# A short-band attention branch whose two key blocks are joined before the softmax and parted again behind the transposes

## The chip, the cores and the metric

The kernel runs on one NeuronCore of one Trainium2 chip. The metric is the device time of one execution in microseconds (us), the median of several runs. A profile of one further execution shows what each engine did when: TensorE (PE, with its weight loads as PEld), VectorE (DVE), ScalarE (ACT), GpSimd (POOL) and the DMA queue of SyncE (SP).

## What is computed

One decoder layer over 1024 tokens of width 1024. It has two attention mixers beside each other: mixer A (three branches, long) and mixer B, the short band: 8 query heads over 2 key heads, head width 64, a causal window of 128 keys, ALiBi and one sink per head. The change is in mixer B alone. Cut to that, the reference is:

```python
def banded_attention(q, k, v, slopes, window, sinks):      # window = 128, Q_BLOCK = 128
    # a block of 128 queries sees its own 128 keys and the 128 before them
    s = einsum('bgrnqd,bgnkd->bgrnqk', qb, kb) * (dh ** -0.5)
    dist = qpos[:, :, None] - kpos[:, None, :]
    valid = (dist >= 0) & (dist < window) & (kpos[:, None, :] >= 0)
    s = s - slopes * dist
    s = where(valid, s, NEG)
    p = softmax(concatenate([s, sink], axis=-1), axis=-1)[..., :-1]
    return einsum('bgrnqk,bgnkd->bgrnqd', p, vb)
```

With a window of exactly 128, query p of a block sees key j of its own block where j <= p, and key j of the block ahead where j > p. For each j exactly one of the two is seen: 128 keys in all, in 256 columns of which half are masked.

## The kernel before

All products are made in float32 from a rounded high part and a low part (names `..h` and `..l`, or `wh`, `wl`), so one projection of 128 rows takes three matmuls for each of 8 slices.

**Stages.** First the input projections, then the attention: four units in the order (B, 0), (B, 1), (A, 0), (A, 1), one per mixer and key head `g`. A unit of mixer B runs over 8 query tiles `i` of 128 tokens, with one branch "swa"; a unit of mixer A has three branches for each tile. At the end come the two output projections. Between the attention's matmuls stand projections for later stages (matmuls into `b_pj`). They need weights that are loaded by SP, rounded by ACT (`wh`, L161) and subtracted by POOL (`wl`, L164).

**One tile of the short band.** `scores` makes, for each of 4 heads `r`, a score product of two matmuls (L770 with `kh`, L773 with `kl`) into one of three PSUM banks `b_s`, 256 columns wide for i > 0 (both key blocks beside each other). VectorE's reduce (L780) scales it, adds the distance table, writes the row to `ps` or `pw` and keeps the minimum (scores are held negated). ACT takes the exponential (L792, with its sum), and after the sink (L798 to L801) POOL scales the four rows (L804). `weigh` then goes over the key blocks: four transposes by matmul with the identity into `b_pt` (L841), ACT rounds them to `ph` (L847), VectorE subtracts to `pl` (L848), and two matmuls of 512 columns (L849, L852) add the block's values into `b_pv`. So a tile with i > 0 has 8 transposes, two pairs of `ph` and `pl`, and 4 products. `finish` copies `b_pv` (L861 on ACT, L862 on VectorE) to the one buffer `ot`, POOL multiplies it by the gate path (L863), and SP stores it. `b_pv` has one bank, so a tile's first product waits for L862 of the tile before.

**What sets the order.** The program's text order only gives priorities. A scheduler lays each engine's instructions in a fixed row, by its own estimate of durations; on the chip every engine takes its row in order and waits with semaphores. `scores` of tile i+1 and `weigh` of tile i are written beside each other at high priority, the projections fill in. A counter of TensorE columns (`mark`, `done`) paces the projections: `whole` holds each unit's estimate, and `hold` keeps a projection behind a chosen matmul. `chain` keeps instructions of one kind in their written order.

## Time and profile before

| what | value |
|---|---|
| time, median of 3 runs | 908.1 us (908.0 to 910.78) |
| profiled execution: its own time | 909.31 us |
| profiled execution: its span, first to last instruction | 907.5 us |
| PE busy | 894.1 us, 99% of the span |
| VectorE, ScalarE, GpSimd busy | 554.3, 505.3 and 352.8 us |
| stretch of the short band's scaled rows, 173.7 to 299.3 us | PE busy 125.6 of 125.6 us; GpSimd 78.16 us |

PE's busy share counts matmuls from start to modelled end, and they overlap; what a matmul costs the row of PE is the step from its start to the next start, as the chain of work shows it. A wait of PE shows as idle time with a releaser behind it. The profiled execution is 1.2 us above the median, and its span 0.6 us below.

### The profile page before, as it was taken

Reading aid. Unit: us, or ns where it says so; the run is one execution under the profiler, and the core shown is the slowest. Engines: PE = TensorE matmul, PEld = TensorE weight load, DVE = VectorE, ACT = ScalarE, POOL = GpSimd, SP = SyncE. Lnnn points to the kernel's source line nnn. Section 1 sums busy time; section 2 is a strip of 40 time slices with the busy share of each in tenths; the row PEclk is TensorE's granted clock in tenths of the full one; section 3 lists DMA queues with packets and bytes.
Section 4 is the critical chain, followed back from the end, with each engine's and each line's share of the span. In section 5 each row is a group of like instructions: output and inputs, shape, how many; then the busy total and the mean of one; then the engine's idle time right before and its main releaser. Section 6 shows DMA issues by size and latency. Waiting matters only on the chain.

```text
span 907.5 us, 14317 instructions
## 1 busy us (share of the span) xinstructions
PE 894.1 (99%) x4568; PEld 755.8 (83%) x4568; DVE 554.3 (61%) x1546; ACT 505.3 (56%) x1151; POOL 352.8 (39%) x422
## 2 busy tenths in 40 slices
PE   9999999999999999999999999999999999999997
PEld 8889888888888878888888878888887888887885
DVE  5866864475577787675576687566464372677322
ACT  5476732476676767665656667565564564441111
POOL 0000411364675866443545566453442375200000
PEclk9999999999999999999999999999999999999999
DMA  8872442333233312111211211111202587334422
GB/s 313 299 262 69 140 159 85 117 94 105 83 105 101 98 51 69 59 44 64 70 47 60 70 55 63 59 47 60 81 30 77 204 259 228 104 113 184 137 95 88
DMA packets 63870, 100.84 MB, mean 111 GB/s; under 512 B 7473, under 2 KB 24241, under 8 KB 63794
## 3 DMA queue, kind: packets, MB, share of 16 engines
q1 hardware_dynamic: 62640, 98.69, 32.9%
q10 hardware_dynamic: 1154, 1.23, 0.4%
q8 instruction: 36, 0.59, 0.3%
q14 instruction: 40, 0.33, 0.1%
HBM read 79.97 MB, written 19.92 MB: 110 GB/s over the span
## 4 chain that ended last, share of the span: by engine, by line
PE 94%; DVE 3%; ACT 1%; issue 1%; DMA 0%; POOL 0%; DVEq 0%; POOLq 0%; ACTq 0%
PE b_pt L841 8%; PE b_pj L900 7%; PE b_pj L904 7%; PE b_pj L905 7%; PE b_pj L194 5%; PE b_pj L195 5%; PE b_pj L187 5%; PE b_s L773 4%; PE b_s L770 4%; PE b_pv L852 4%; PE b_pv L849 4%; PE b_s L1140 1%; PE b_s L1139 1%; PE b_s L1141 1%; PE b_pt L294 1%; PE b_s L210 1%
## 5 line engine op out<-in xcount | busy, mean ns | idle before, releaser
L164 POOL TENSOR_TENSOR wl<-wraw,wh 128x512 fp32r<-128x512 f32 x102 | 132.8, 1305 | 140.2 <-ACT wh L161 91.9
L848 DVE TENSOR_TENSOR pl<-b_pt,ph 128x512 fp32r<-128x512 f32 x162 | 110.3, 686 | 55.5 <-ACT ph L847 54.6
L847 ACT CAST ph<-b_pt 128x512 fp32r<-128x512 f32 x162 | 93.5, 584 | 63.5 <-PE b_pt L841 52.7
L900 PE MATMUL b_pj<-hh,wh 128*128 128x512 f32 x288 | 117.1, 410 | 0.0
L905 PE MATMUL b_pj<-hh,wl 128*128 128x512 f32 x288 | 113.8, 395 | 0.0
L904 PE MATMUL b_pj<-hl,wh 128*128 128x512 f32 x288 | 113.3, 395 | 0.0
L195 PE MATMUL b_pj<-hh,wl 128*128 128x512 f32 x240 | 94.6, 394 | 0.0
L187 PE MATMUL b_pj<-hh,wh 128*128 128x512 f32 x240 | 94.5, 394 | 0.0
L194 PE MATMUL b_pj<-hl,wh 128*128 128x512 f32 x240 | 94.2, 392 | 0.0
L804 POOL TENSOR_SCALAR ps<-ps,rr,gates 128x128 f32<-128x128 f32 (+7 forms) x64 | 52.5, 822 | 94.6 <-DVE rr L796 50.0
L770 PE MATMUL b_s<-kh,q 128*128 128x256 f32 (+6 forms) x272 | 85.8, 322 | 0.0
L792 ACT ACTIVATE ps<-ps,mins 128x256 f32<-128x256 f32 (+7 forms) x96 | 64.9, 678 | 36.6 <-DVE mins L780 32.3
L773 PE MATMUL b_s<-kl,q 128*128 128x256 f32 (+6 forms) x272 | 83.8, 316 | 0.0
L161 ACT CAST wh<-wraw 128x512 fp32r<-128x512 f32 x94 | 57.8, 617 | 39.2 <-PE b_pj L194 13.6
L792 ACT ACTIVATE pw<-pw,mins 128x256 f32<-128x256 f32 (+4 forms) x96 | 60.7, 634 | 23.9 <-DVE mins L780 23.6
L849 PE MATMUL b_pv<-ph,V 128*128 128x512 f32 x162 | 65.5, 404 | 3.5 <-DVE ot L862 3.5
L852 PE MATMUL b_pv<-pl,V 128*128 128x512 f32 x162 | 67.9, 419 | 0.3
L905 PEld LDWEIGHTS b_pj<-hh,wl 128*128 128x128 f32 x288 | 54.1, 188 | 10.8
L863 POOL TENSOR_TENSOR ot<-ot,zt 64x512 f32<-64x512 f32 x32 | 41.7, 1303 | 55.0 <-DVE ot L862 43.5
L904 PEld LDWEIGHTS b_pj<-hl,wh 128*128 128x128 f32 x288 | 54.3, 189 | 8.8
L900 PEld LDWEIGHTS b_pj<-hh,wh 128*128 128x128 f32 x288 | 53.8, 189 | 7.8
L804 POOL TENSOR_SCALAR pw<-pw,rr,gates 128x640 f32<-128x640 f32 (+4 forms) x64 | 47.2, 741 | 31.7 <-DVE rr L796 28.6
(298 smaller groups left out, 2138.8 us busy)
## 6 DMA issues: line engine op xcount, KB each, us to landing
wraw<-in_w_blk SPq DMA_DIRECT2D x90, 256.0 KB, 2.9
wa<-in_w_adaT SPq DMA_DIRECT2D x24, 512.0 KB, 5.6
w1raw<-in_w SPq DMA_DIRECT2D x16, 256.0 KB, 3.2
od<-ot SPq DMA_DIRECT2D x64, 64.0 KB, 2.1
sp_MA<-sp SPq DMA_DIRECT2D x16, 256.0 KB, 2.0
wraw<-in_w_o SPq DMA_DIRECT2D x16, 256.0 KB, 3.0
wraw<-in_w_out SPq DMA_DIRECT2D x16, 256.0 KB, 3.4
t<-od SPq DMA_DIRECT2D x16, 256.0 KB, 3.9
```

Of the source, the lines that this page charges most:

```text
L164: chain("wl", nc.gpsimd.tensor_tensor(wl, raw, wh.bitcast(F32), ALU.subtract))
L187: ins = nc.tensor.matmul(t, lhsT=wh, rhs=hh[kc][half], start=(kc == 0), stop=False)
L194: nc.tensor.matmul(t, lhsT=wh, rhs=hl[kc][half], start=False, stop=False)
L195: nc.tensor.matmul(t, lhsT=wl, rhs=hh[kc][half], start=False, stop=(kc == KC - 1))
L770: ins = nc.tensor.matmul(sp[:, :n_in], lhsT=q, rhs=rh, start=True, stop=False)
L773: nc.tensor.matmul(sp[:, :n_in], lhsT=q, rhs=rl, start=False, stop=True)
L792: nc.scalar.activation(rows[r][:, :off], rows[r][:, :off], AF.Exp, scale=-1.0, bias=last_min[:, r : r + 1], accum_out=sums[:, r : r + 1])
L848: nc.vector.tensor_tensor(pl, t, ph.bitcast(F32), ALU.subtract)
L852: nc.tensor.matmul(pv, lhsT=v, rhs=pl, start=False, stop=(last and n == len(todo) - 1))
L900: ins = nc.tensor.matmul(self.t, lhsT=wh, rhs=hh[kc][self.half], start=(kc == 0), stop=False)
L904: nc.tensor.matmul(self.t, lhsT=wh, rhs=hl[kc][self.half], start=False, stop=False)
L905: ins = nc.tensor.matmul(self.t, lhsT=wl, rhs=hh[kc][self.half], start=False, stop=(kc == KC - 1))
```

## The change

For tiles with i > 0 of mixer B, the two key blocks share one 128-column row. The table `DB` becomes 128 wide: column j holds p - j where j <= p, and p - j + 128 where j > p; beside it lies a mask `first` that is 1 where j > p. After the score product, VectorE copies the block ahead's columns over the own block's where the mask is set (`copy_predicated`, in the PSUM bank), and the reduce, the exponential and POOL's scaling run over 128 columns. The new `weigh_joined` makes four transposes for both blocks, one rounding and one subtraction into the two halves of a tile `own`; POOL then makes two selections by position over all 1024 columns: `ahead` (key > query, else 0) and, in place, `own` (key <= query, else 0). Four products of 512 columns follow. The two tiles come from the ring `ps`, and the four rows of a task are parts of one `pw` buffer. The column counts of the pacing go from 4096 to 3100 for such a tile.

```diff
-            tables["DB"] = tab[:, :256]
+            tables["DB"] = tab[:, :P]
+            tables["first"] = tab[:, P : 2 * P].bitcast(mybir.dt.int32)
...
-            "slc": ("ps", S), "win": ("pw", 640), "cmp": ("pc", 0), "swa": (("ps", S), ("pw", 640))[i % 2]}[br]
+            "slc": ("ps", S), "win": ("pw", 640), "cmp": ("pc", 0), "swa": ("pw", 640)}[br]
+        if br == "swa":
+            four = at.tile([P, width], F32, name=tag, tag=tag, bufs=4)
...
-                row = at.tile([P, width], F32, name=tag, tag=tag, bufs=4)
+                row = four[:, r * P : r * P + P] if br == "swa" else at.tile([P, width], F32, name=tag, tag=tag, bufs=4)
...
-                        d0 = (b0 - (i - 1)) * P
-                        dist = tables["DB"][:, d0 : d0 + w]
+                        dist = tables["DB"]
...
+                    if br == "swa" and i:
+
+                        nc.vector.copy_predicated(sp[:, P : 2 * P], tables["first"], sp[:, :P])
+                        pre, w = P, P
                     ins = nc.vector.tensor_tensor_reduce(
                         out=row[:, off : off + w], in0=sp[:, pre : pre + w], in1=dist, scale=2.0 ** -(h + 1),
...
+    def weigh_joined(g, i, rows, pv):
+
+        pump()
+        t = bank("pt")
+        for r in range(4):
+            ins = nc.tensor.transpose(t[:, r * P : r * P + P], rows[r][:, :P], ident)
+            if r == 0:
+                chain("pt", ins)
+                mark(ins, 3100)
+        own, ahead = (at.tile([P, S], F32R, name="pj", tag="ps", bufs=4) for _ in range(2))
+        nc.scalar.copy(own[:, :512], t)
+        nc.vector.tensor_tensor(own[:, 512:], t, own[:, :512].bitcast(F32), ALU.subtract)
+
+        nc.gpsimd.affine_select(
+            out=ahead, in_=own.bitcast(F32), pattern=[[0, 8], [-1, P]], compare_op=ALU.is_gt, fill=0.0,
+            base=0, channel_multiplier=1)
+        nc.gpsimd.affine_select(
+            out=own, in_=own.bitcast(F32), pattern=[[0, 8], [1, P]], compare_op=ALU.is_ge, fill=0.0,
+            base=0, channel_multiplier=-1)
+        for n, (part, b) in enumerate(((ahead, i - 1), (own, i))):
+            v = V[b][:, 4 + g].rearrange("p a d -> p (a d)")
+            for k in range(2):
+                ins = nc.tensor.matmul(
+                    pv, lhsT=v, rhs=part[:, 512 * k : 512 * k + 512], start=(n == 0 and k == 0),
+                    stop=(n == 1 and k == 1))
...
-    d = 128 + p - j
-    DB = dist(d, (d < 0) | (d >= 128))
+    j = np.arange(P)[None, :]
+    DB = np.concatenate([np.where(j > p, p - j + P, p - j), j > p], axis=1).astype(np.float32)
```

The scheduler lays all rows of the short band anew; from about tile 2 of unit (A, 0) on, the rows of all engines are again those of before. Three places follow.

PE in unit (B, 0), the transposes of a tile with two blocks (before: `ps` rows into the banks `b_pt_2432` and `b_pt_2443`; `b_pj` is a projection, `b_s` a score of a later tile):

```order
L841 MATMUL b_pt_2432<-ident_70,ps_2289 128x128
L841 MATMUL b_pt_2443<-ident_70,ps_2289 128x128
L841 MATMUL b_pt_2432<-ident_70,ps_2295 128x128
L841 MATMUL b_pt_2443<-ident_70,ps_2295 128x128
L841 MATMUL b_pt_2432<-ident_70,ps_2301 128x128
L841 MATMUL b_pt_2443<-ident_70,ps_2301 128x128
L770 MATMUL b_s_2546<-kh_873,q_2188 128x128
L841 MATMUL b_pt_2432<-ident_70,ps_2307 128x128
L841 MATMUL b_pt_2443<-ident_70,ps_2307 128x128
L773 MATMUL b_s_2546<-kl_874,q_2188 128x128
```

The same tile of the changed kernel, on PE:

```order
L839 MATMUL b_pt_2401<-ident_70,pw_2263 128x128
L194 MATMUL b_pj_2333<-hl7_116,wh_2329 128x512
L839 MATMUL b_pt_2401<-ident_70,pw_2263 128x128
L195 MATMUL b_pj_2333<-hh7_100,wl_2330 128x512
L839 MATMUL b_pt_2401<-ident_70,pw_2263 128x128 x2
L187 MATMUL b_pj_2437<-hh0_86,wh_2429 128x512
L194 MATMUL b_pj_2437<-hl0_102,wh_2429 128x512
L195 MATMUL b_pj_2437<-hh0_86,wl_2430 128x512
```

Eight transposes have become four; score matmuls, projections and the four products into `b_pv` are as many as before.

POOL early in unit (B, 0) before, where L804 scales a tile's four rows, L863 is the gate product and L164 a projection's low part:

```order
L804 TENSOR_SCALAR pw<-pw,rr 128x256 x4
L164 TENSOR_TENSOR wl<-wraw,wh 128x512 x2
L804 TENSOR_SCALAR ps<-ps,rr 128x256 x4
L863 TENSOR_TENSOR ot<-ot,zt 64x512
L164 TENSOR_TENSOR wl<-wraw,wh 128x512 x2
L863 TENSOR_TENSOR ot<-ot,zt 64x512
L804 TENSOR_SCALAR pw<-pw,rr 128x256 x4
```

The same engine and place in the changed kernel (L847 makes `ahead`, L850 makes `own`, both in tiles named `pj`; L810 is the scaling, L900 the gate product):

```order
L810 TENSOR_SCALAR pw<-pw,rr 128x128 x4
L900 TENSOR_TENSOR ot<-ot,zt 64x512
L847 AFFINE_SELECT pj<-pj 128x1024
L164 TENSOR_TENSOR wl<-wraw,wh 128x512
L850 AFFINE_SELECT pj<-pj 128x1024
L164 TENSOR_TENSOR wl<-wraw,wh 128x512
L847 AFFINE_SELECT pj<-pj 128x1024
L810 TENSOR_SCALAR pw<-pw,rr 128x128 x4
L850 AFFINE_SELECT pj<-pj 128x1024
L164 TENSOR_TENSOR wl<-wraw,wh 128x512 x2
L900 TENSOR_TENSOR ot<-ot,zt 64x512
```

Two selections per tile now stand between the scalings, the gate products and the low parts of the weights.

PE at the change from unit (B, 1) to unit (A, 0), before: the last transpose of the short band's last tile (bank `b_pt_3333`), then the products of the tile ahead of it and a projection. The last tile's own first product comes 20 rows below the first row shown:

```order
L841 MATMUL b_pt_3333<-ident_70,pw_3275 128x128
L852 MATMUL b_pv_3289<-pl_3296,V5_134 128x512
L849 MATMUL b_pv_3289<-ph_3306,V6_135 128x512
L852 MATMUL b_pv_3289<-pl_3307,V6_135 128x512
L904 MATMUL b_pj_3371<-hl3_109,wh_3107 128x512
L905 MATMUL b_pj_3371<-hh3_93,wl_3108 128x512
L900 MATMUL b_pj_3371<-hh4_95,wh_3111 128x512
L904 MATMUL b_pj_3371<-hl4_111,wh_3111 128x512
L905 MATMUL b_pj_3371<-hh4_95,wl_3112 128x512
L770 MATMUL b_s_3395<-kh_2979,q_3248 128x192
```

The same place in the changed kernel (the last tile's bank is `b_pt_3239`, its `ahead` is `pj_3245`; the `b_s` are scores of unit A's first tile):

```order
L839 MATMUL b_pt_3239<-ident_70,pw_3180 128x128
L856 MATMUL b_pv_3213<-pj_3220,V5_134 128x512 x2
L856 MATMUL b_pv_3213<-pj_3219,V6_135 128x512 x2
L772 MATMUL b_s_3305<-kh_2914,q_3171 128x192
L775 MATMUL b_s_3305<-kl_2915,q_3171 128x192
L772 MATMUL b_s_3313<-kh_2914,q_3174 128x192
L775 MATMUL b_s_3313<-kl_2915,q_3174 128x192
L772 MATMUL b_s_3328<-kh_2922,q_3026 128x128
L775 MATMUL b_s_3328<-kl_2923,q_3026 128x128
L856 MATMUL b_pv_3238<-pj_3245,V6_135 128x512 x2
L772 MATMUL b_s_3335<-kh_2922,q_3029 128x128
```

Between the last transpose and the last tile's first product there are now four products and six score matmuls, and no projection.

## Rows read from the trace of the kernel before

**Rows 1.** Page, part 1 (busy us per engine) and part 4 (chain).

```profile
PE 894.1 (99%) x4568; PEld 755.8 (83%) x4568; DVE 554.3 (61%) x1546; ACT 505.3 (56%) x1151; POOL 352.8 (39%) x422
...
PE 94%; DVE 3%; ACT 1%; issue 1%; DMA 0%; POOL 0%; DVEq 0%; POOLq 0%; ACTq 0%
```

**Rows 2.** Busy us by stretch: PE, PEld, DVE, ACT, POOL, PE clock, DMA share, GB/s.

```profile
173.70:299.30 125.60, 125.60 (x666) 106.61 (x666) 83.80 (x247) 84.87 (x228) 78.16 (x103) 1.00 0.31 96
```

**Rows 3.** Chain of work, 160 to 330 us: start, us, what; steps of PE.

```profile
184.03 0.23 PE b_pv L849
...
185.17 0.44 PE b_pt L841 x4
```

**Rows 4.** Timeline of PE: start, duration, instruction; a score's two matmuls.

```profile
180.85 0.28 PE L770 MATMUL b_s<-kh,q 128*128 128x256 f32 x1
180.97 0.28 PE L773 MATMUL b_s<-kl,q 128*128 128x256 f32 x1
```

**Rows 5.** Groups by form, 174 to 300 us, PE: count | busy us, mean ns.

```profile
L841 PE MATMUL b_pt<-ident,pw 128*128 128x128 f32 x56 | 9.7, 272 | 0.0
```

**Rows 6.** Groups by form, 173.7 to 299.3 us, POOL.

```profile
L164 POOL TENSOR_TENSOR wl<-wraw,wh 128x512 fp32r<-128x512 f32 x25 | 32.1, 1290 | 6.7 <-ACT wh L161 6.7
L863 POOL TENSOR_TENSOR ot<-ot,zt 64x512 f32<-64x512 f32 x14 | 18.1, 1290 | 22.8 <-DVE ot L862 15.0 <-DVE rr L798 4.3 <-DVE minc L786 1.7
L804 POOL TENSOR_SCALAR pw<-pw,rr 128x256 f32<-128x256 f32 x32 | 14.7, 479 | 10.3 <-DVE rr L801 8.5 <-PE b_pv L852 1.8
...
L804 POOL TENSOR_SCALAR ps<-ps,rr 128x128 f32<-128x128 f32 x8 | 2.8, 372 | 8.8 <-ACT pw L792 6.2 <-PE b_pt L841 2.6
```

**Rows 7.** Groups by form, whole span, POOL: the only selection, and scalings by width.

```profile
L804 POOL TENSOR_SCALAR ps<-ps,rr,gates 128x1024 f32<-128x1024 f32 x8 | 9.6, 1202 | 23.6 <-DVE rr L796 19.3 <-DMA wraw<-in_w_blk 2.2 <-PE b_pj L904 2.1
...
L804 POOL TENSOR_SCALAR ps<-ps,rr,gates 128x128 f32<-128x128 f32 x8 | 3.5, 443 | 7.5 <-PE b_pt L841 7.5
...
masks.py:199 POOL TENSOR_SCALAR_AFFINE_SELECT ident<-ident 128x128 f32<-128x128 f32 x1 | 0.3, 292 | 0.1
```

**Rows 8.** Groups by form, 174 to 300 us, DVE and ACT.

```profile
L848 DVE TENSOR_TENSOR pl<-b_pt,ph 128x512 fp32r<-128x512 f32 x28 | 18.8, 681 | 2.4 <-ACT ph L847 2.2
...
L847 ACT CAST ph<-b_pt 128x512 fp32r<-128x512 f32 x28 | 15.8, 586 | 1.7 <-PE b_pt L841 1.1 <-PE b_pv L849 0.2
...
L780 DVE CUSTOM_DVE_ANT_0 pw<-b_s,tab,nsink 128x256 f32<-128x256 f32 x30 | 13.6, 476 | 12.5 <-PE b_s L773 10.0 <-PE b_pt L841 1.6 <-POOL ps L804 0.9
...
L862 DVE TENSOR_TENSOR ot<-b_pv,ot 64x512 f32<-64x512 f32 x14 | 9.5, 680 | 4.1 <-ACT ot L861 4.0
...
L780 DVE CUSTOM_DVE_ANT_0 ps<-b_s,DC,nsink 128x128 f32<-128x128 f32 x4 | 1.4, 344 | 2.2 <-PE b_s L773 2.1
...
L780 DVE CUSTOM_DVE_ANT_0 ps<-b_s,DC 128x128 f32<-128x128 f32 x2 | 0.5, 288 | 1.2 <-PE b_pt L841 1.2
L786 DVE CUSTOM_DVE_ANT_0 pc<-b_s,tab 128x63 f32<-128x63 f32 x2 | 0.4, 214 | 1.0 <-DMA tab<-in_DA 1.0
```

**Rows 9.** Groups by form, 0 to 160 us, DVE: a plain copy out of PSUM.

```profile
L635 DVE COPY kcf<-b_pt 128x126 f32<-128x126 f32 x1 | 0.3, 289 | 1.2 <-PE b_pt L632 1.2
```

**Rows 10.** Line L800 (ns min/median/max), and timeline rows of DVE and POOL at 195 us.

```profile
L800 DVE TENSOR_TENSOR sums<-sums,rr x16: 148/164/1716, 173.2 to 292.7; 128x4 f32<-128x4 f32 x16
...
195.60 1.29 POOL L863 TENSOR_TENSOR ot<-ot,zt 64x512 f32<-64x512 f32 x1 [4.28 <-DVE rr L798]
...
196.11 0.80 DVE L800 TENSOR_TENSOR sums<-sums,rr 128x4 f32<-128x4 f32 x1
```

**Rows 11.** Timeline at the change of units: start, duration, instruction.

```profile
300.49 1.03 PE L841 MATMUL b_pt<-ident,pw 128*128 128x128 f32 x8
301.28 0.48 PE L852 MATMUL b_pv<-pl,V 128*128 128x512 f32 x1
...
304.69 0.48 PE L849 MATMUL b_pv<-ph,V 128*128 128x512 f32 x1
```

**Rows 12.** Timeline of PE in unit (A, 0): its longest idle time.

```profile
337.39 0.50 PE L849 MATMUL b_pv<-ph,V 128*128 128x512 f32 x1 [1.80 <-DVE ot L862]
```

More of the change, by code (lines that the diff above doesn't have):

```diff
@@ L826, in weigh_pairs @@
                     start=False, stop=(n == 1 and r == 1))
+    def weigh_joined(g, i, rows, pv):
[21 more added lines that the diff above has]
+                    stop=(n == 1 and k == 1))
+                if n == 0 and k == 0:
+                    chain("pv", ins)
     def weigh(mixer, g, i, br, tiles, pv, first, last):
@@ L832, in weigh @@
             weigh_pairs(g, rows, pv)
+            return
+        if br == "swa" and i:
+            weigh_joined(g, i, rows, pv)
             return
```

6 lines of the change are left out of this document (3 added, 3 removed).

## The prediction, made before the changed kernel ran

> **What bounds the kernel now.** I read the page's busy times and its chain first. PE is busy for 894.1 us of 907.5, and 94% of the chain that ended last is PE [rows 1]. So a change counts by what it does to PE's row: work taken out of it shortens the time, and a wait put into it lengthens it. Then I cut out the stretch of the short band by windows. From 173.7 to 299.3 us PE is busy for all of its 125.60 us, VectorE for 83.8, ScalarE for 84.9, GpSimd for 78.2, at full clock [rows 2]. PE never waits there: projections fill what the attention leaves open. GpSimd has 47 us to spare, VectorE 42.
>
> PE's groups by form give 272 ns for a transpose, in two groups of 56, of which one is shown [rows 5]. That is not its price, since matmuls overlap. The chain has the price: four transposes in a row take 0.44 us, 0.11 each, and a 512-column product 0.23 [rows 3]; the two matmuls of a 256-column score start 0.12 apart [rows 4].
>
> **What leaves PE.** 14 tiles have two blocks (7 in each of two units). Each loses 4 of 8 transposes: 56 x 0.11 = 6.2 us. The four products of 512 columns and the scores stay. With PE without a gap this is 6.2 us off the time; it is the whole gain, 0.7%.
>
> **VectorE and ScalarE.** VectorE gets 56 masked copies of 128 columns out of PSUM. The trace has none; the nearest are a plain copy out of PSUM of 126 columns, 289 ns [rows 9], and the 256-column reduce, 476 ns [rows 8], as the upper end. I take 0.29, since the copy is of the same size and source: +16.2 us. Against it, 56 reduces fall from 476 to about 344 ns (the 128-column one with the sink), -7.4, and 14 subtractions of 681 ns go, -9.5 [rows 8]. Sum -0.7 us, at the upper end +9.8, against 42 idle. ScalarE only loses work (14 roundings of 586 ns [rows 8], and narrower exponentials). Neither becomes a bound; these edits cost nothing while PE has other work in its row.
>
> **GpSimd, the open price.** It gets 28 selections of 128x1024. Its work now is 78.2 us [rows 2], and the scaling of 56 rows falls from about 478 to 372 ns [rows 6], -5.9: 72.3 us remain, plus 28 X. The trace has one selection, of 128x128: 292 ns [rows 7]. For X the lower end is that row plus 896 more columns at the slope of the scaling, (1202 - 443)/896 = 0.85 ns a column: 292 + 759 = 1.05 us. The upper end is 292 ns for each of the eight 128-column pieces, 2.34 us. I take 1.05 to 1.3: going from one to two scalar tensors raises the 128-column scaling from 372 to 443 ns [rows 6, 7], so one with none would take about 300, and the selection's 292 is as much, which speaks for the same slope. Then GpSimd has 72.3 + 28 x 1.05 = 101.7 us (at 1.3, 108.7) to do in a stretch of 125.6 - 6.2 = 119.4 us. It fits, with 85 to 91% busy.
>
> [...]
>
> **Is the longer way through GpSimd hidden?** From a tile's last transpose to its first product the way is now: end of the matmul after its slot (272 - 110 = 0.16), rounding 0.59, subtraction 0.68, selection 1.05: 2.5 us. GpSimd's row can put one low part (1.29), one gate product (1.29) and four scalings (1.49) ahead of the selection: 6.6 us. In the changed row of PE the work between these two points, counted with 0.23, 0.12 and 0.11, is 7.1 to 11.5 us in 13 of the 14 tiles, and 8.3 to 12.0 us to the first product of `own`. So PE finds both selections done. If that cover were gone, each tile would stop PE by the difference. The ring `ps` holds two tiles' pairs: a rounding waits for the products of two tiles ahead, which end some 12 us behind their transposes, while two tiles take 2 x 119.4/14 = 17 us, so that wait costs nothing.
>
> **Where it is not hidden.** The last tile of the short band has only four products and six narrow scores in that place: 4 x 0.23 + 6 x 0.11 = 1.6 us. The kernel before has 304.69 - 301.28 = 3.4 us there, all filled, with no stop [rows 11]. Now count from the end of the last transpose's slot. The subtraction starts at 0.16 + 0.59 and ends at 1.43, the selection at 2.5. Behind the subtraction, in VectorE's row, stand the first two minima of unit A and their compressed partners, 2 x (0.29 + 0.21) = 1.0, and then the 0.68 of L862's successor, which frees `b_pv` [rows 8]: end at 3.1, at 2.8 if they overlap as such pairs do. PE arrives at 1.6, so it stops for 1.2 to 1.5 us. The score behind it needs a bank that VectorE frees after two more minima, a reciprocal or two and another compressed one, 0.7 to 1 us. Of that and of later banks I count 1.0. Together 2.4 us, between 0.9 (the selection's way alone) and 4 (unit A's first transposes, which wait for GpSimd behind `own` and a gate product, stop PE too).
>
> The stop of 1.80 us in unit (A, 0) [rows 12] has a cause that the change leaves (a bank freed by L862); I keep it, with 2 us either way in the range.
>
> **Sum.** -6.2 + 2.4 = -3.8 us. On the profiled execution's own time, 909.31 -> 905.5; its span 907.5 -> 903.7. The median of the runs is 908.1, 1.2 below the profiled one, and the forecast goes by the median: 904.3.
>
> **A rule that speaks against it.** VectorE's small add L800, from two SBUF tensors, takes 164 ns in the median and up to 1716; one of 0.80 us starts inside a gate product of GpSimd and ends with it, 195.60 + 1.29 = 196.89 [rows 10]. So such adds wait for GpSimd's running instruction. The changed kernel has GpSimd busy more of the time. 28 adds (L798 and L800 of 14 tiles) of at most 1.55 us extra make 43 us, about all of VectorE's idle time, but one tile's share, 3.1 us, lies in the way from the minimum to the scaling, where PE has projections. The masked copy and the reduce read one operand from PSUM. [...]
>
> **Rivals.**
> - GpSimd becomes the bound: slower. If X is well above 1.3, GpSimd's row is longer than PE's. At X = 1.9 its sum is 72.3 + 53.2 = 125.5 us, the stretch of before: from there on the kernel is slower. At 2.34 it is 137.8, 12.2 more than before: 920.3. A middle, X = 2.1, gives 131.1: 913.6. For it: no wide selection is in the trace, and GpSimd takes its row in order, so waits add to the sum. Against it: the 292 ns, and that GpSimd's rows of before show plain prices by column. Chance 0.17.
> - The gain is given back at the change of units: no change. [...] 906 to 908.1; I put it at 907. Chance 0.27.
> - Hardly any stop (0.5 us), and the one of [rows 12] halved too: 908.1 - 6.2 + 0.5 - 0.9 = 901.5. Chance 0.10.
> - That the change doesn't do what it says is no rival of weight: the transposes are gone from PE's row.
>
> **How the numbers follow.** The forecast (0.46) and the fast rival (0.10) are below 905.4, faster by over 0.3%, which is about what a measurement of this kernel can tell from no change: 0.56. Within 0.3% (905.4 to 910.8): 0.27. Slower: 0.17. The range leaves out the fast rival's lower half and the GpSimd rival above X = 2.05: 901.0 to 912.0.
>
> **What will show each step.** PE's busy time in the short band and its transposes (56 fewer, 0.11 each in the chain); the duration of the 128x1024 selection (right if 1.0 to 1.3 us); GpSimd's busy share in the stretch, some 85%; the masked copy near 0.29 us; PE without a stop in the stretch up to the last tile, and there one to three stops of 1 to 4 us in all, ended by VectorE (`b_pv` or `b_s`) or POOL. It is wrong if a selection takes over 1.9 us, if PE stops on `pj` in the middle of the stretch, or if the copy out of and into PSUM takes 0.5 us or more, so that scores wait for their banks.

## The result: slower, and the profile after

The changed kernel takes 913.8 us in the median, against 908.1 before: a ratio of 1.0059, with a 95% interval of 1.0046 to 1.0072. The forecast was 904.3 in a range of 901.0 to 912.0. The transposes left PE as forecast, and 11 us of stops and of lower clock came in their place.

The page of the changed kernel (span 909.7 us, its own time 911.4): part 1, busy us per engine, and part 4, the chain. They answer [rows 1].

```profile
PE 889.4 (98%) x4512; PEld 748.0 (82%) x4512; DVE 564.0 (62%) x1588; ACT 493.4 (54%) x1137; POOL 378.4 (42%) x450
...
PE 88%; DVE 6%; ACT 2%; DMA 1%; issue 1%; POOL 1%; SPq 0%; DVEq 0%; POOLq 0%; ACTq 0%
```

PE is busy 4.7 us less (56 matmuls fewer), and the kernel is slower all the same: PE's share of the chain fell from 94 to 88%, and VectorE's rose from 3 to 6%.

One thing has to be taken out before the two traces can be compared. Full clock was granted from 4.6 us of the span in this profiled run, from 13.1 in that of before, and the first product of the values (L210) started at 13.80 against 16.93 us. That is no effect of the change: e_last_old, a joined kernel whose edit leaves the prologue as it is, had its first one at 17.45. I therefore measure from that product's start to the last matmul's start: 883.7 us before, 889.2 after, 5.6 more, as the medians say (5.7).

PE's waits of the changed kernel, 160 to 345 us: who waits, for whom, us in all, times, the longest. Before has one wait of 1 us or more in this stretch, the 1.80 us of [rows 12].

```profile
PE b_pv L856 <- DVE rr L802: 2.7, 1, 2.7
PE b_s L772 <- DVE minc L792: 2.2, 3, 1.7
PE b_pj L187 <- DVE kl L508: 1.7, 1, 1.7
PE b_pv L886 <- DVE ot L899: 0.5, 1, 0.5
```

To see all of it, I took for each matmul the time to the next one's start, less the median for its shape (512 columns 0.227, a transpose 0.108), and summed what is above zero:

| surplus of PE's row, us | 160 to 296 | 296 to 312 | 312 to 345 | 345 to 700 |
|---|---|---|---|---|
| before | 5.4 | 0.6 | 4.4 | 22.1 |
| after | 9.1 | 7.3 | 5.2 | 21.4 |

Behind 700 us it is 0.6 more after. Together +11.1 us; less the transposes' 6.2 that is 4.9, near the 5.6 measured. So 3.7 us went in the short band, and 6.7 at the change from unit (B, 1) to unit (A, 0).

**The short band.** VectorE, GpSimd and PE of the changed kernel around 190 us (start, us, instruction, idle time before it and its releaser):

```profile
186.12 3.94 DVE L504 CAST kl<-kl 128x128 fp32r<-128x128 f32 x1
190.20 0.69 DVE L508 TENSOR_TENSOR kl<-b_pj,kh 64x512 fp32r<-64x512 f32 x1
...
185.18 1.46 POOL L900 TENSOR_TENSOR ot<-ot,zt 64x512 f32<-64x512 f32 x1
186.59 1.09 POOL L847 TENSOR_SCALAR_AFFINE_SELECT pj<-pj 128x1024 fp32r<-128x1024 f32 x1
187.65 1.28 POOL L164 TENSOR_TENSOR wl<-wraw,wh 128x512 fp32r<-128x512 f32 x1
188.89 1.10 POOL L850 TENSOR_SCALAR_AFFINE_SELECT pj<-pj 128x1024 fp32r<-128x1024 f32 x1
...
190.95 0.50 PE L187 MATMUL b_pj<-hh,wh 128*128 128x512 f32 x1 [1.70 <-DVE kl L508]
```

A cast of 128x128 from SBUF to SBUF, 0.23 us in the median of its line, takes 3.94. It started within GpSimd's gate product, and three more GpSimd instructions followed without a gap: selection, low part, selection. It ended with the last of them (188.89 + 1.10 = 189.99; 186.12 + 3.94 = 190.06). Behind it in VectorE's row stood L508, which frees a `b_pj` bank, and PE stopped 1.70 us for that bank. The bank was not late for want of VectorE's time, but because VectorE was held by GpSimd's row. After this there are three small waits of scores for their banks (0.2 to 0.4 us at 220 to 280 us).

Before, the same cast was held too, but by one GpSimd instruction (a low part, 188.02 to 189.30), and PE did not stop:

```profile
188.24 1.15 DVE L504 CAST kl<-kl 128x128 fp32r<-128x128 f32 x1
```

**The change of units.** PE, VectorE, GpSimd, SyncE's queue and ScalarE of the changed kernel:

```profile
298.93 0.28 PE L775 MATMUL b_s<-kl,q 128*128 128x192 f32 x1
300.87 0.33 PE L772 MATMUL b_s<-kh,q 128*128 128x192 f32 x1 [1.66 <-DVE minc L792]
304.31 1.19 PE L856 MATMUL b_pv<-pj,V 128*128 128x512 f32 x2 [2.74 <-DVE rr L802]
306.57 0.63 PE L942 MATMUL b_pj<-hh,wl 128*128 128x512 f32 x1
...
299.68 0.69 DVE L845 TENSOR_TENSOR pj<-b_pt,pj 128x512 fp32r<-128x512 f32 x1 [0.57 <-ACT pj L844]
300.29 0.28 DVE L786 CUSTOM_DVE_ANT_0 ps<-b_s,DC 128x128 f32<-128x128 f32 x1
303.48 0.68 DVE L899 TENSOR_TENSOR ot<-b_pv,ot 64x512 f32<-64x512 f32 x1 [2.40 <-ACT ot L898]
...
297.49 1.29 POOL L164 TENSOR_TENSOR wl<-wraw,wh 128x512 fp32r<-128x512 f32 x1
298.73 1.26 POOL L900 TENSOR_TENSOR ot<-ot,zt 64x512 f32<-64x512 f32 x1
...
300.02 1.25 SPq L903 DMA_DIRECT2D od<-ot  x2
...
298.41 0.62 ACT L161 CAST wh<-wraw 128x512 fp32r<-128x512 f32 x1
299.06 0.58 ACT L844 CAST pj<-b_pt 128x512 fp32r<-128x512 f32 x1
302.86 0.58 ACT L898 COPY ot<-b_pv 64x512 f32<-64x512 f32 x1 [3.21 <-DMA od<-ot]
```

The first stop (1.66) is for a score bank: the minima of unit A's first scores stand in VectorE's row behind the joined subtraction L845, which waits for the rounding L844. That one started 0.98 us after the last transpose's end (297.81 + 0.27 = 298.08), because ScalarE's row had a rounding for a projection (L161) ahead of it. The second (2.74) is put down to L802, but it ends 0.15 us after L899, which frees `b_pv`. L899 waited for the copy into the one `ot` buffer, that for the store of the tile ahead, and that for its gate product, which GpSimd began at 298.73, behind four scalings, a selection and a low part.

Behind the stops comes a third loss. Windows of the changed kernel (us of PE, PEld, DVE, ACT, POOL busy, then PE's granted clock, DMA share, GB/s):

```profile
174.61:289.08 114.47, 111.85 (x566) 92.40 (x565) 87.85 (x265) 66.90 (x199) 89.15 (x114) 1.00 0.29 93
289.08:310.25 21.17, 16.77 (x78) 13.87 (x77) 11.53 (x46) 11.57 (x36) 18.85 (x25) 0.84 0.36 110
302.00:309.00 7.00, 4.69 (x15) 3.86 (x15) 2.37 (x17) 4.61 (x19) 5.86 (x11) 0.54 0.31 93
```

From 301.58 us on, the trace's clock record grants 0.50 of full speed for 6.83 us, and 1.00 ahead of that and behind it. Of this PE worked 304.31 to 308.41 at the lower level. A 512-column matmul takes 0.63 there and starts 0.43 after the one ahead of it (306.57, 307.00), against 0.39 and 0.227 else. By that I estimate the cost at about half of these 4.1 us, 2 us. The same windows show where GpSimd's work went: 78% busy in the short band (89.15 of 114.47), 89% in the 21 us behind it.

### The profile page after: what moved, and what is told of

It is laid out like the page before. It is cut to its first block, busy times and chain, and to the rows that moved or that the text cites. A ratio compares the mean times of both kernels' runs of the same rounds, so it can differ in the third digit from the quotient of the medians.

```text
span 909.7 us, 14222 instructions
## 1 busy us (share of the span) xinstructions
PE 889.4 (98%) x4512; PEld 748.0 (82%) x4512; DVE 564.0 (62%) x1588; ACT 493.4 (54%) x1137; POOL 378.4 (42%) x450
## 4 chain that ended last, share of the span: by engine, by line
PE 88%; DVE 6%; ACT 2%; DMA 1%; issue 1%; POOL 1%; SPq 0%; DVEq 0%; POOLq 0%; ACTq 0%
PE b_pj L937 7%; PE b_pj L941 7%; PE b_pj L942 7%; PE b_pt L878 6%; PE b_pj L194 5%; PE b_pj L187 5%; PE b_pj L195 5%; PE b_s L772 4%; PE b_s L775 4%; PE b_pv L889 3%; PE b_pv L886 3%; PE b_s L1179 1%; PE b_s L1178 1%; PE b_s L1177 1%; PE b_s L210 1%; PE b_s L1099 1%
## 5 line engine op out<-in xcount | busy, mean ns | idle before, releaser
L164 POOL TENSOR_TENSOR wl<-wraw,wh 128x512 fp32r<-128x512 f32 x102 | 133.7, 1314 | 137.6 <-ACT wh L161 89.4
L885 DVE TENSOR_TENSOR pl<-b_pt,ph 128x512 fp32r<-128x512 f32 x134 | 91.5, 688 | 55.0 <-ACT ph L884 54.1
L884 ACT CAST ph<-b_pt 128x512 fp32r<-128x512 f32 x134 | 77.7, 583 | 64.0 <-PE b_pt L878 50.8
L810 POOL TENSOR_SCALAR ps<-ps,rr,gates 128x128 f32<-128x128 f32 (+7 forms) x64 | 52.5, 823 | 95.5 <-DVE rr L802 49.8
L798 ACT ACTIVATE pw<-pw,mins 128x128 f32<-128x128 f32 (+4 forms) x128 | 70.0, 548 | 40.1 <-DVE mins L786 38.0
L161 ACT CAST wh<-wraw 128x512 fp32r<-128x512 f32 x94 | 57.6, 615 | 32.5 <-PE b_pj L941 11.8
L798 ACT ACTIVATE ps<-ps,mins 128x128 f32<-128x128 f32 (+7 forms) x64 | 49.6, 777 | 26.9 <-DVE mins L786 23.4
L772 PEld LDWEIGHTS b_s<-kh,q 128*128 128x128 f32 x272 | 51.4, 189 | 12.5 <-issue 2.8
L810 POOL TENSOR_SCALAR pw<-pw,rr,gates 128x640 f32<-128x640 f32 (+4 forms) x64 | 47.2, 742 | 33.9 <-DVE rr L802 26.5
L900 POOL TENSOR_TENSOR ot<-ot,zt 64x512 f32<-64x512 f32 x32 | 41.5, 1297 | 41.1 <-DVE ot L899 28.4
L775 PEld LDWEIGHTS b_s<-kl,q 128*128 128x128 f32 x272 | 51.5, 189 | 7.1
```

The costliest lines, as they stand in the source:

```text
L164: chain("wl", nc.gpsimd.tensor_tensor(wl, raw, wh.bitcast(F32), ALU.subtract))
L772: ins = nc.tensor.matmul(sp[:, :n_in], lhsT=q, rhs=rh, start=True, stop=False)
L775: nc.tensor.matmul(sp[:, :n_in], lhsT=q, rhs=rl, start=False, stop=True)
L798: nc.scalar.activation(rows[r][:, :off], rows[r][:, :off], AF.Exp, scale=-1.0, bias=last_min[:, r : r + 1], accum_out=sums[:, r : r + 1])
L810: nc.gpsimd.tensor_scalar(rows[r][:, :off], rows[r][:, :off], rr[:, r : r + 1], gate, ALU.mult, ALU.mult)
L885: nc.vector.tensor_tensor(pl, t, ph.bitcast(F32), ALU.subtract)
```

## The experiments

What each theory says. Theory 1: most of the loss is at the change of units, from GpSimd's row (late gate product) and VectorE's. Theory 2: GpSimd's selections hold VectorE's casts and adds between SBUF tensors, all through the short band. Rivals: the pacing, which now has 3100 columns to a tile in place of 4096, left no projection there; and, from the prediction, GpSimd becomes the bound. Times are medians; the kernel before was measured again beside each group of runs (908.1 to 909.1 in the median), so runs of different groups are compared by their ratios. "body" is the profiled run from the first product of the values to the last matmul (before 883.7, after 889.2; ratio after 1.0059).

| kernel | us | ratio to before, 95% interval | body, us |
|---|---|---|---|
| e_last_old | 912.7 | 1.0035 (1.0021 to 1.0050) | 888.3 |
| e_pace | 910.6 | 1.0015 (1.0001 to 1.0028) | 885.9 |
| e_casts_act | 905.7 | 0.9955 (0.9940 to 0.9971) | 880.5 |
| e_no_select | 905.4 | 0.9963 (0.9949 to 0.9977) | 880.1 |
| e_kb_casts | 911.6 | 1.0019 (1.0008 to 1.0031) | 884.2 |
| e_pace_casts | 907.6 | 0.9983 (0.9973 to 0.9993) | 884.0 |
| e_before_casts | 905.8 | 0.9953 (0.9936 to 0.9969) | 880.7 |
| e_adds_pool | 907.8 | 0.9988 (0.9978 to 0.9998) | 884.9 |
| e_gate_dve | 912.1 | 1.0028 (1.0014 to 1.0042) | 889.3 |
| e_last_casts | 906.0 | 0.9965 (0.9953 to 0.9978) | 881.3 |
| e_last2_casts | 905.3 | 0.9961 (0.9947 to 0.9974) | 880.6 |
| e_sel_twice | 912.6 | 1.0042 (1.0026 to 1.0058) | 888.5 |
| e_all_before | 905.1 | 0.9955 (0.9941 to 0.9969) | 879.6 |
| e_all_joined | 904.1 | 0.9955 (0.9939 to 0.9971) | 881.3 |
| e_all_last | 900.7 | 0.9920 (0.9905 to 0.9935) | 877.9 |
| e_all_last2 | 905.5 | 0.9954 (0.9939 to 0.9969) | 879.8 |

**Selections left out**, `e_no_select`:

```diff
-        nc.gpsimd.affine_select(out=ahead, ...)
-        nc.gpsimd.affine_select(out=own, ...)
-        for n, (part, b) in enumerate(((ahead, i - 1), (own, i))):
+        for n, (part, b) in enumerate(((own, i - 1), (own, i))):
```

> Both selections are left out of the computation: the products of the two blocks read the same joined weights, so GpSimd loses 28 x 1.09 = 30.5 us and everything else stays. If GpSimd carries the loss, by the port (theory 2) and by its queue (the late gate product behind selections, theory 1), all of it goes: 913.8 - 10 = 903 to 905. If the stops at the change of units come from VectorE's minima, or from the pacing that leaves no projection there, only the 3.7 us of the port come back: 910.

905.4, at the edge of what theories 1 and 2 together said. The body is 9.1 us below the changed kernel's, more than the whole loss; the stop at 190 us, the small ones and the half clock are gone, and at the change of units 2.4 us of surplus are left of 7.3. So GpSimd's two selections a tile carry the loss. The rest of the joining (copy, narrower minima, fewer transposes) is a gain, of 3.4 us by the ratio and 3.6 by the body where the transposes alone are worth 6. The cast L504 stands on VectorE here too, and without the selections it is held by the end of a gate product and one low part, without a stop of PE:

```profile
189.16 1.83 DVE L504 CAST kl<-kl 128x128 fp32r<-128x128 f32 x1
```

The port of this expectation is theory 2's name for VectorE's casts and adds that end with an instruction of GpSimd (3.94 us at 186.12); what the two engines share there no run shows. By which road the selections cost is for the next runs: the planner laid PE's row anew from 188 us on in this kernel, so it does not part the roads.

**The casts**, `e_casts_act` and, for one key block, `e_kb_casts`:

```diff
-                nc.vector.tensor_copy(khp[:, :P], before[0][:, HS - P :].bitcast(F32))
+                nc.scalar.copy(khp[:, :P], before[0][:, HS - P :].bitcast(F32))
...
-            dve(nc.vector.tensor_copy(kh[o0:o1, :], hi.bitcast(F32)))
...
+            if keys[0] == ("swa", 0) and half or keys[0] == ("slc", 0) and not half:
+                nc.scalar.copy(kh[o0:o1, :], hi.bitcast(F32))
```

The condition of e_kb_casts is `keys[0] == ("swa", 0) and half` alone.

> Joined, but the SBUF-to-SBUF casts of the key blocks formed in the short band (six casts of each of two blocks) run on ScalarE in place of VectorE. Theory 2 (VectorE's 128x128 cast of 3.94 us waits until GpSimd, busy with select, low part, select, goes idle): the 1.70 us stop at 190.95 us is gone and 1.7 to 2.0 us come back, about 911.9. Rival (the stop there is the bank's late release by VectorE's queue in general): the stop stays at 1 us or more, 913 or above. Neither touches the change of units; if the two stops there shrink too, VectorE's row there was also late from a cast.

905.7: 8 us by the medians (9.4 by the ratios, 8.7 by the bodies) where 2 were expected. The stop at 190 us and the small ones are gone, as theory 2 says. But more has gone, at the change of units (surplus 4.4 in place of 7.3) and in unit A (the stop of 1.69 us at 540.79). The planner had moved PE's row as well, so I took one block alone.

> Only the key block of mixer B (formed at 185 to 192 us) has its casts on ScalarE; PE's order at the change of units stays as in the changed kernel, without a projection between the last tile's transposes and its products' first half. Theory 2 (the 3.94 us cast alone stops PE there): the stop of 1.70 us is gone, the two stops at the change of units stay at about 1.7 and 2.7 us, 913.8 - 2 = 911.8, or 909.5 where the clock doesn't fall behind them. Rival (that cast had delayed VectorE's row up to the change of units): the later stops shrink too, 906 to 908.

911.6, the 911.8 of theory 2 (by the ratios 3.6 us are gained). PE's waits in e_kb_casts, 160 to 345 us:

```profile
PE b_pv L860 <- DVE rr L806: 2.9, 1, 2.9
PE b_s L776 <- DVE minc L796: 2.2, 3, 1.6
```

No wait for `b_pj` is left. PE's row differs from the changed kernel's only between 186 and 204 us, both stops of the change of units stand as they were, and the half clock comes again (298.61 us, 6.83 us long). Counted up to the first of these stops, the short band's surplus is 5.6 us, against 9.1 after and 5.4 before; at the change of units it is 7.3 as after. So the short band's loss and that of the change of units are two things, and the cast made only the first. The edit did more than its expectation says: it also moved the casts of the window's second halves in units A, and there the stop at 541 us, a surplus of 1.86 us, is gone too. (Its profiled execution took 907.0 us, the shortest of the twelve, so its body is no measure of the median.)

That led back to the kernel before. 

> The kernel before, with the casts of the two key blocks on ScalarE and nothing else changed. Theory 2 (the casts cost only where the selections fill GpSimd's row): no change within 0.1%, 908 to 909, since PE has no stop from them there. Rival (the casts on ScalarE are a gain of their own, which has nothing to do with the joined tiles): 1 to 3 us faster, 906 to 907.5, and the joined tiles are worth that much less.

905.8: the rival held (4.3 us by the ratio, 3.0 by the body). The stop of 1.80 us in [rows 12], and a like one at 538 us, are gone in that run. In the trace of before, VectorE and GpSimd ahead of that stop:

```profile
331.44 1.68 DVE L503 CAST kh<-kh 128x128 fp32r<-128x128 f32 x1
336.66 0.68 DVE L862 TENSOR_TENSOR ot<-b_pv,ot 64x512 f32<-64x512 f32 x1
...
331.75 1.29 POOL L164 TENSOR_TENSOR wl<-wraw,wh 128x512 fp32r<-128x512 f32 x1
```

A cast of the same kind, held until a low part of GpSimd ended (331.75 + 1.29 = 333.04; 331.44 + 1.68 = 333.12), put VectorE's row late, with the L862 that PE waited for in it: VectorE has no gap between the two. The cast was held for 1.45 of the 1.80 us; the rest is the casts' own time, which the edit takes off VectorE's row as well. So of the 8.7 us of e_casts_act by the bodies, 3.0 (by the ratios 4.3 of 9.4) are a gain that has nothing to do with joining. The fair question is joined against not joined with the casts moved in both: 905.7 against 905.8, nothing.

**The small adds.** `e_adds_pool`, on top of e_casts_act:

```diff
-            nc.vector.tensor_tensor(rr, last_min, nsink[:, 4 * g : 4 * g + 4], ALU.subtract)
+            nc.gpsimd.tensor_tensor(rr, last_min, nsink[:, 4 * g : 4 * g + 4], ALU.subtract)
...
-            nc.vector.tensor_tensor(sums, sums, rr, ALU.add)
+            nc.gpsimd.tensor_tensor(sums, sums, rr, ALU.add)
```

> Joined, casts on ScalarE, and the two small adds of a tile's sink (128x4, two operands in SBUF) moved from VectorE to GpSimd's own row: no instruction of VectorE between minimum and scaling then waits for GpSimd. With the casts alone moved the adds still took 20.4 us together where before it was 10.6. If their waits cost nothing, as the prediction has it: 905 to 906.5. If they hold VectorE's row and so the score banks (stops of 0.36 and 0.56 us at 296 us, 0.9 us in the short band): 904 to 905.

907.8, slower than either. The adds took 0.20 us each on GpSimd, but they and what waited for them stretched its row, and a stop of 3.88 us for `b_pv` ended at 298.87 us. In e_casts_act the adds still took 20.4 us, and its surplus up to 296 us (6.0) is hardly above that of before (5.4); with the adds moved it is 6.0 as well, up to that stop. So held adds cost next to nothing in the short band. A longer row of GpSimd does cost, at the end.

**The change of units.** First the last tile the old way, `e_last_old`, and the pacing, `e_pace`:

```diff
+    def joined(g, i, br):
+        return br == "swa" and (g, i) != (1, 7)
...
-        if br == "swa" and i:
+        if joined(g, i, br) and i:
             weigh_joined(g, i, rows, pv)
```

> The last tile of unit (B, 1) goes the old way (two blocks, eight transposes, no selection, no masked copy); the other 13 tiles stay joined. Theory 1 (most of the loss is the two stops of 1.66 and 2.74 us at the change of units and the 1.2 GHz stretch behind them, some 6.7 us together): the stops and the slow stretch are gone, the time falls from 913.8 to about 907.5 (6.7 back, 0.4 lost on four transposes). Theory 2 (the loss is VectorE's casts and small adds waiting for GpSimd all through the short band, 3.7 us, and the slow stretch by chance): 913 or a little less, and the stop of 1.70 us at 190.95 us stays under both.

912.7. The slow stretch of both theories is the one of granted clock 0.50; the traces give a share of full speed and no frequency. The surplus at the change of units is 3.3 in place of 7.3, but 0.7 more lies behind it, four transposes are back, and in this run a half clock of 3.41 us came at 543.2, behind a stop of 1.70 us. The stop in the short band stays (1.74 us), as both theories said. The body is 0.9 below the changed kernel's, the ratio 0.24% lower: a part of theory 1, less than half of what it said.

```diff
-                mark(ins, 3100)
+                mark(ins, 4096)
...
-                weighed = 1650 if br == "cmp" else 3100 if br == "swa" and i else 2048 * nb
+                weighed = 1650 if br == "cmp" else 2048 * nb if br == "swa" else 2048 * nb
```

> Joined as in the changed kernel, but the short band's tiles are counted with the columns of the kernel before (4096 a tile in place of 3100) in the pacing of the projections, which puts six projection matmuls (6 x 0.23 = 1.4 us) between the last tile's neighbours at the change of units. Rival of theory 1 (the stops there come from the pacing, which leaves no projection, and not from the longer way through GpSimd and VectorE): at least 4 of the 6.7 us come back, 908 to 910. Theory 1 as it stands (late gate product on GpSimd, VectorE's row): the projections fill 1.4 us of 4.4, the clock falls as before, 911.5 to 913.

910.6, between the two; the ratio is 0.44% lower, 4 us, as the rival said. Six projection matmuls lie ahead of the last tile's first product, the stop of 2.74 is gone, one of 1.42 for the score bank remains, and no half clock follows. The gate product still stands behind two selections and a low part (298.30 us). So the pacing was a part of the loss: with 3100 columns a tile no projections are left there to hide the late release.

> Both edits: pacing by 4096 columns a tile, and all casts of the two key blocks of the short band on ScalarE. If they cure different stops (the casts those of 189 and 276 to 283 us, the pacing those at the change of units) and the run with all casts moved still has some of the latter: 904 to 905.5. If the casts alone had cured both, the pacing adds nothing: 905.7 as with the casts alone.

907.6, worse than the casts alone: a stop of 2.34 us for the score bank and a half clock. The two cures do not add, since each moves PE's row at the change of units.

So I looked for an edit that leaves PE's row as it is. `e_gate_dve` has the row of the changed kernel up to 309 us, past both stops; behind that the planner laid it anew:

```diff
-        nc.gpsimd.tensor_tensor(ot, ot, zt.rearrange("d r t -> d (r t)"), ALU.mult)
+        eng = nc.vector if mixer == "B" and g == 1 and i >= 5 else nc.gpsimd
+        eng.tensor_tensor(ot, ot, zt.rearrange("d r t -> d (r t)"), ALU.mult)
```

> As the changed kernel, PE's row the same word for word up to the change of units and beyond, but the gate products of the last three tiles of unit (B, 1) run on VectorE. Theory 1a (the stop of 2.74 us is the chain late gate product on GpSimd, store of ot, copy into ot, release of b_pv): that stop shrinks to under 1 us, and about 2 us of it and some of the clock's fall behind it come back: 909 to 911.5. [...]

PE and ScalarE of e_gate_dve at the change of units:

```profile
301.89 0.50 PE L772 MATMUL b_s<-kh,q 128*128 128x192 f32 x1 [2.05 <-DVE minc L792]
302.87 1.19 PE L856 MATMUL b_pv<-pj,V 128*128 128x512 f32 x2
...
301.43 0.58 ACT L898 COPY ot<-b_pv 64x512 f32<-64x512 f32 x1 [0.88 <-DMA od<-ot]
```

The copy waits 0.88 us for the store in place of 3.21, and PE's stop for `b_pv` is gone: the chain from the late gate product to `b_pv` (1a) is shown. The median, 912.1, lies 0.6 us above the 909 to 911.5 of theory 1a; the ratio is 0.3% lower, near 2.8 us. The stop for the score bank stays (2.05), and the half clock too, 6.8 us long, with more of PE's work in it: the surplus at the change of units falls only from 7.3 to 6.1. The profiled run shows no shorter body, since behind 309 us the stop of [rows 12] is back and a second half clock (3.41 us at 540 us) fell into it.

Then the dose: `e_sel_twice` repeats the second selection, with the casts on ScalarE.

```diff
         nc.gpsimd.affine_select(
             out=own, in_=own.bitcast(F32), pattern=[[0, 8], [1, P]], compare_op=ALU.is_ge, fill=0.0, ...)
+        nc.gpsimd.affine_select(
+            out=own, in_=own.bitcast(F32), pattern=[[0, 8], [1, P]], compare_op=ALU.is_ge, fill=0.0, ...)
```

> Casts on ScalarE, and the selection of own made twice (it changes nothing the second time): GpSimd gets 14 x 1.09 = 15.3 us more in a stretch where it has then about 118 us of work for 113 to 119 us. Rival of the prediction (GpSimd becomes the bound): PE stops for pj in the middle of the stretch, 2 to 8 us slower than 905.7, 908 to 914. If GpSimd's row still hides: 905.7 to 907.

912.6: 7 us more by the medians, 7.9 by the ratios, for 15.3 us of GpSimd. PE's waits in e_sel_twice, 160 to 345 us:

```profile
PE b_pv L863 <- DVE ot L906: 7.1, 2, 3.7
```

The amount was right and the place was not. PE did not stop in the middle of the stretch; GpSimd's backlog came out at the change of units, at `b_pv`, as two stops of 3.4 and 3.7 us, with a half clock of 13.65 us around and behind them.

**What is left, and a faster kernel.** All casts moved in both kernels (`e_all_before`, `e_all_joined`), then one and two old tiles at the end.

> The kernel before with the SBUF-to-SBUF casts of every key block that is formed during attention on ScalarE (the earlier variant left those of unit A's second halves and of the last unit's block on VectorE). It is the control for the next three: what remains of the casts' stops in units A goes, 905.8 or a few tenths less.

> The changed kernel with the same casts moved. No cast of VectorE can wait for GpSimd any more in either, so the difference to the control is the joined tiles with GpSimd's row alone. If GpSimd's backlog at the change of units gives the gain back (3 to 6 us there): within 1.5 us of the control, 904.5 to 906.5, with its excess between 294 and 345 us. If the casts were the whole of it: 6 us below the control, 899.5.

Level by the ratios, both 0.9955; by the bodies the joined kernel is 1.7 us slower. In e_all_before no wait of PE shows between 160 and 700 us. PE's waits in e_all_joined, 160 to 345 us:

```profile
PE b_s L776 <- DVE minc L796: 0.9, 3, 0.4
PE b_pv L860 <- POOL pj L854: 0.6, 1, 0.6
PE b_pv L890 <- DVE ot L903: 0.5, 1, 0.5
PE b_s L776 <- DVE mins L790: 0.4, 1, 0.4
```

Its surplus over the control, each stop counted where it ends, is 0.3 us up to 296, 4.7 at the change of units (with 3.41 us of half clock) and 1.8 from there to 345. So the change of units and what follows it give the gain of 6.2 back even where no cast is held. One of these stops, 0.62 us at 296.05, is for a selection (`pj`): there the way through GpSimd itself is not hidden.

> Last tile of unit (B, 1) the old way, and all casts of the two key blocks on ScalarE. If the two cures add (the last tile's 3.4 us at the change of units and the 3 us of the casts in the short band, on a kernel whose units A also gain 1.6 us twice from the casts): the body falls below the kernel before with moved casts (905.8) by up to 13 x 0.44 = 5.7 us, 901 to 904. If the selections of the tiles ahead of the last one already make GpSimd's row late there: 905 to 906, as with the casts alone.

906.0, no better than the casts alone: the surplus at the change of units fell to 2.4, but a cast that I had left on VectorE (2.71 us long from 323.01 on, under two low parts) stopped PE for 2.76 us up to 326.37.

> The last two tiles of unit (B, 1) the old way, and the casts on ScalarE. If GpSimd's row (its selections back to back) is what is late at the change of units, two old tiles let it run empty, and the stops there fall to under 1 us together: 12 x 0.44 = 5.3 us below 905.8, less 1: 901 to 902.5. If the stops there are VectorE's minima or the order of the projections, they stay at 3 us: 903.5 to 905.

905.3, a miss. GpSimd's row did run empty (2.4 us idle ahead of 295.4), and another wait took the place: PE stopped 2.87 us up to 300.00 for a score bank that L801 frees. VectorE of e_last2_casts:

```profile
299.61 0.23 DVE L801 CUSTOM_DVE_ANT_0 pc<-b_s,tab 128x63 f32<-128x63 f32 x1 [0.71 <-DMA tab<-in_DA]
```

Mixer A's table lies in the place of the short band's, so its load waits for the last minimum of unit (B, 1), which ended at 296.59; the load was issued at 296.65. The next two kernels load the compressed masks early:

```diff
+    tab = at.tile([P, HS + P], F32, name="tab")
     def load_tables(mixer):
-        tab = at.tile([P, HS + P], F32, name="tab", tag="tab", bufs=1)
...
-            nc.scalar.dma_start(tab[:, : HS + 120], io["DA"])
+            nc.scalar.dma_start(tab[:, HS : HS + 120], io["DA"][:, HS : HS + 120])
+            nc.scalar.dma_start(tab[:, :HS], io["DA"][:, :HS])
```

> As the run ahead, but the last tile of unit (B, 1) goes the old way, and the masks of mixer A's table have a place of their own beside the short band's table, so that the compressed ones are loaded early. Backlog theory: GpSimd loses two selections where it is late; the stops at the change of units fall to 1 to 2 us, 13 x 0.44 = 5.7 us less 1.5: 901 to 903. If the stops come from VectorE's row behind the joined subtraction, not from GpSimd: 904 to 905.5.

> The last two tiles the old way, the rest as the run ahead. With the table's split the stop of 2.87 us behind the load of mixer A's table (seen where two tiles were old and the table had one place) is gone: 12 x 0.44 = 5.3 us below the control, less at most 1: 900.5 to 902. If it stays at 904 or above, neither the table nor GpSimd's row was the cause of what is left there.

e_all_last takes 900.7, just under the 901 to 903 of the backlog theory, with a ratio of 0.9920, whose interval lies below that of the control: joined tiles with an old one at the end, the casts on ScalarE and the table split beat both kernels. Against e_all_before this is 3.2 us by the ratios, 1.7 by the bodies. The 1.7 is the better figure: full clock was granted from 5.1 us on in the profiled execution of e_all_last, from 12.95 in that of the control, and the times of both kernels lie in two groups some 3 us apart, of which the lower has four of six executions here and one of five there. Group against group the gap is 2.0 and 1.8 us. Its PE waits, 160 to 345 us:

```profile
PE b_pv L897 <- ACT ph L895: 0.8, 1, 0.8
PE b_pt L889 <- POOL pw L821: 0.5, 1, 0.5
PE b_pt L889 <- POOL pc L821: 0.4, 1, 0.4
PE b_pv L841 <- ACT ph L836: 0.2, 1, 0.2
```

e_all_last2 is a miss, 905.5: PE stopped 1.74 us, at the last tile's transposes, for GpSimd's scalings, and a half clock came. GpSimd had been idle for 2.75 us up to 296.7, so it was no backlog. The planner had put twelve projection matmuls behind that tile's first two transposes, and none in the 6 us ahead of them.

## Why the prediction was wrong, point by point

- **What leaves PE: right.** 56 transposes are gone, at 0.108 us in place of the 0.11 taken, and where the selections are left out 3.4 to 3.6 of these 6 us show.
- **Prices: right.** The selections, VectorE's copy and the adds of the changed kernel, by form, 174 to 300 us (busy us, mean ns):

```profile
L850 POOL TENSOR_SCALAR_AFFINE_SELECT pj<-pj 128x1024 fp32r<-128x1024 f32 x13 | 14.4, 1108 | 0.2
...
L786 DVE CUSTOM_DVE_ANT_0 pw<-b_s,tab,nsink 128x128 f32<-128x128 f32 x53 | 17.6, 346 | 0.8
L784 DVE COPY_PREDICATED b_s<-tab,b_s 128x128 f32<-128x128 int32 x53 | 14.5, 288 | 4.4 <-PE b_s L775 4.1
L804 DVE TENSOR_TENSOR rr<-mins,nsink 128x4 f32<-128x4 f32 x15 | 10.9, 726 | 0.3
L806 DVE TENSOR_TENSOR sums<-sums,rr 128x4 f32<-128x4 f32 x15 | 9.9, 657 | 2.8 <-ACT rr L805 2.6
```

  1.1 us for a selection (1.05 to 1.3 forecast) and 0.288 for the copy (0.29): the slope of [rows 7] held. GpSimd's groups in this window sum to 101.9 us, against 101.7 forecast.
- **The cover in the middle: right.** PE waits on no `pj` there, and no such wait appeared even with a third selection. But "PE without a stop in the stretch up to the last tile" was wrong: it stopped 1.70 us for `b_pj`.
- **"A rule that speaks against it": the first step that failed.** It had from [rows 10] that an add of VectorE from two SBUF tensors ended with GpSimd's gate product (0.80 us at 195.60), but it counted this only for the 28 adds, and only until GpSimd's running instruction ends. The adds rose by 10 us together and cost next to nothing, as said. The masked copies and the reduces, with one operand in PSUM, show no hold in the changed kernel: 274 to 297 ns for the 56 of L784, 331 to 353 for the 57 of L786 in the short band. The casts stood in no term of the sum, though [rows 12] hung on one that stood held for 1.45 us in the same trace; and the wait lasted over several GpSimd instructions that followed without a gap: the 3.94 us at 186.12 span three changes of instruction in GpSimd's row, and the cast got its turn at none of them. Why not, no run shows. Put at nothing, this cost 3.7 us in the short band (with the score banks' small waits). "These edits cost nothing while PE has other work in its row" stands for VectorE's own edits: e_no_select keeps them all and is faster than the kernel before.
- **"Where it is not hidden", 2.4 us (0.9 to 4): the place was right, the path to `b_pv` and the size were not.** The surplus there measured 6.7 us. A stop for a score bank was priced at 1.0, behind the last tile's product; it measured 1.66 and came ahead of that product, with the rounding L844 0.98 us late in ScalarE's row, which the count had left out. For `b_pv` I followed the selection and VectorE's row, 1.2 to 1.5 us; what ended it was the store of `ot`, 2.74 us. GpSimd's longer row delays the gate product, the store starts late, and with one `ot` buffer the next tile's copy waits (3.21 us at 302.86). The one buffer entered no term of the count. The clock's fall behind the stops, 2 us, was not foreseen.
- **The stop of [rows 12] "has a cause that the change leaves": wrong.** The cause is the cast; in the changed kernel the stop split into 0.49 and 0.51 us as the order around it moved, and in e_gate_dve it is back. (PE's rows of the two kernels differ up to about 386 us, further than the section on the change says.)
- **The sign of being wrong.** None of the three that were named came (a selection of 1.9 us, a stop on `pj` in the middle, a copy of 0.5 us). All three asked for the price of the new work; none asked what it does to instructions that the edit leaves alone.
- **The rivals.** "The gain is given back at the change of units" was the right case as to place, with a chance of 0.27, and even its 906 to 908.1 was too low against the measured 913.8: the runs showed a surplus of 6.7 us at the change of units, with two stops of 1.66 and 2.74 us in it, and of 3.7 in the short band. "GpSimd becomes the bound" was wrong as a mechanism for the middle, but e_sel_twice shows what it looks like: two stops of 3.4 and 3.7 us at the end.

What stays open: which wait ends last at the change of units differs with each order of PE's row (score bank, `b_pv`, the table, the transposes), and I have no single cause for all of them; what they share is that the last tile's way through four engines has little of PE's own work beside it. e_all_last differs from e_all_joined in two edits, the old tile and the table, which were not run apart. In e_before_casts the hold of the casts and their own time on VectorE were not parted either. Why the clock falls behind some stops and not behind others is not shown.

## What to carry to other kernels

Busy shares do not tell whether work can be moved onto GpSimd: GpSimd was 78% busy in the short band here, and a cast of VectorE took 3.94 us in place of 0.23 beside it. List VectorE's instructions that read and write SBUF, look in the trace for those that take many times their median, and see what PE waits for behind them. Work added to GpSimd came out at the change of a stage here (15.3 us more of it in e_sel_twice, stops of 3.4 and 3.7 us there), in instructions that the edit doesn't touch (a gate product, its store and one buffer; 2.74 us in the changed kernel): look there too. And before a gain is credited to an edit, put its side effects into the old kernel too: here 3 of 8.7 us were the casts' alone.

## What the runs showed that I had not expected

- VectorE's wait for GpSimd's SBUF work spanned several instructions. Between 160 and 345 us, casts and adds between SBUF tensors that took 0.9 us or more: 6 in the kernel before, 15 in the changed one, the longest 1.72 and 3.94 us. Each of the 21 ended 0.02 to 0.28 us after the end of a GpSimd instruction. In the changed kernel VectorE got its turn at a change of instruction without a gap in 5 of the 15 cases, and was passed over at one or more of them in 6. VectorE and GpSimd of the changed kernel at 229 us, an add that got its turn behind a low part, and the next one, which a gate product and a low part held:

```profile
228.81 1.09 DVE L804 TENSOR_TENSOR rr<-mins,nsink 128x4 f32<-128x4 f32 x1
230.17 2.22 DVE L806 TENSOR_TENSOR sums<-sums,rr 128x4 f32<-128x4 f32 x1 [0.27 <-ACT rr L805]
...
228.59 1.29 POOL L164 TENSOR_TENSOR wl<-wraw,wh 128x512 fp32r<-128x512 f32 x1
229.84 1.28 POOL L900 TENSOR_TENSOR ot<-ot,zt 64x512 f32<-64x512 f32 x1
231.09 1.28 POOL L164 TENSOR_TENSOR wl<-wraw,wh 128x512 fp32r<-128x512 f32 x1
```
- The granted clock fell to 0.50 of full speed for 3.4 to 13.7 us at the change of units in 9 of the 18 kernels' traces, each time behind or within stops of PE of 0.6 to 4 us, and in three traces for 3.4 us further on, behind stops of 1.7 to 2.8 us. Like stops also went by without it: 1.80 us in the kernel before, 1.42 in e_pace. So a stop's price is not its own length alone: in the changed kernel the half clock put an estimated 2 us on 4.4 us of stops, and in e_pace nothing on 1.42.
- Full clock was granted from 4.1 to 5.1 us of the span on in nine profiled runs, and only from 12.1 to 14.1 us on in the nine others, with the same prologue; the products of the values then start some 3 us later.
